# The table of attention biases is made beside the first norm and stored from 128 partitions instead of 8

## The chip, the cores and the metric

The kernel runs on one core of a Trainium2 chip. The metric is the device time of one execution in microseconds (us). Five engines work side by side, each through its own list of instructions in a fixed order: PE multiplies matrices, ACT (ScalarE), DVE (VectorE) and POOL (GpSimd) compute on the on-chip memory, and SP (SyncE) here only issues transfers (DMAs). An instruction starts when those before it on its engine have been issued and the semaphores it waits for have come.

## The reference, cut to what matters

Two transformer-like blocks follow one another on 1024 tokens of width 1024. The first one normalises `x`, projects it by `w_in`, and feeds two branches: attention in a window, and a state-space scan. Here is the part of it that the change touches:

```
h = rms_norm(x, norm_gain);  q, k, v, ... = split(h @ w_in)
rel  = (arange(384) - 128)[None, :] - arange(128)[:, None]        # key minus query
bias = rel_table[t5_bucket(rel)]                                  # (128, 384, 8 heads)
scores = where(|rel| <= 128 and key in range, q @ k.T / 8 + bias, -1e30)
m = max(scores.max(-1), sink);  p = exp(scores - m)
out = (p / (p.sum(-1) + exp(sink - m))) @ v                       # per block of 128 queries
```

The bias depends on key minus query alone. So for each head one row of 512 numbers (relative positions -255 to 256, with -1e30 where the window ends) holds all of it, and query `q` needs 384 of them from `127 - q` on.

The rest of the first block (gates, scan, merge), the modulation vectors of the second block, and the whole second block (a scan, a short convolution and a layer of experts) follow the same reference in both kernels.

## The kernel before

`phase_a` (L340) does the first block's projections, attention and scan. It loads `x` in eight tiles of 128 tokens (L350). `norm_T` (L303) normalises them in two groups of four tiles and writes the transposed result, split into a high and a low part, as `hTh` and `hTl`: ACT squares and sums (`junk`, L309), DVE finds the inverse roots (`rst`, `rsy`) and scales (`xn`, L315), PE transposes (`nps`, L321), ACT evacuates (`nz`, L324), DVE rounds (`hTh`, L268), POOL subtracts (`hTl`, L269).

The projection takes 34 weight pieces of 512 KB. Each is loaded into one of two `raw` buffers (L258) and split by ACT (`whi`, L266) and POOL (`wlo`, L269); 48 matmuls on it fill two halves of 512 tokens (L277 to L279). Pieces 0 to 5 give `kT`, `v` and the four `qT` (matmuls named `pqkv`); the other 28 (`prest`) are used as filler between the steps of attention and of the scan (`k.fill`).

`attention` (L432) first makes the table. `tab` (32 rows, one more for the mask, by 8 heads) times the one-hot matrix `oh` (33 x 512) gives `pb`, 8 heads x 512 positions; DVE copies it to `fb`. One DMA (L447) stores that to memory as `d_f`, 128 copies of each head's row at a pitch of 513 numbers: 1024 rows of 2 KB, read from 8 partitions. A second DMA (L449) reads `d_f` with the pitch 512, so that partition `q` gets its row shifted by `q`: this is `bt`, 128 x 8 x 384. Every score tile adds its part of `bt` on DVE while it takes the maximum (`sc`, L469).

`modulation` (L840) sums 48 pieces of `ada_w` (512 KB each, two buffers, also named `raw`, L861) on DVE into `ac` (L863), two sums per piece for the first 16 pieces and one for the others; column sums of these (`pm`, L868) go through PE.

The order of instructions on each engine isn't written out by hand. A scheduler takes the program, simulates a timeline of it, and puts each engine's instructions into the order in which the simulation would start them; the order is fixed when the kernel is built. All transfers named here are issued by SP, one after the other.

Of the kernel before, what the change touches and what calls it, by code (L numbers as in the profile page):

```python
# [7 lines left out]
F32 = mybir.dt.float32  # L8
# [4 lines left out]
AF = mybir.ActivationFunctionType  # L13
# [146 lines left out]
class K:  # L160
# [25 lines left out]
    def pool(s, name, side="left", tags=""):  # L186
        return Pool(s.tc, name, side, tags)
# [113 lines left out]
def norm_T(k, pool, xs, ntile, scale, bias, hi, lo):  # L301

    nc = k.nc  # L303
    G = min(4, ntile)
    for g in range(ntile // G):
        ms = pool.tile([128, G], F32, tag=f"nms{G}", name="ms", bufs=2)
        junk = pool.tile([128, 1024], F32, tag="njunk", name="junk", bufs=1)
        for t in range(G):
            nc.scalar.activation(junk, xs[g * G + t], AF.Square, accum_out=ms[:, t:t + 1])  # L309
        nc.vector.tensor_scalar(ms, ms, 1.0 / 1024, 1e-6, op0=OP.mult, op1=OP.add)  # L310
        r = k.rsqrt(pool, ms, G)
        xn = []
        for t in range(G):
            z = pool.tile([128, 1024], F32, tag="nxn", name="xn", bufs=5)
            nc.vector.tensor_scalar(z, xs[g * G + t], r[:, t:t + 1], None, op0=OP.mult)  # L315
            xn.append(z)
        W = 128 * G
        for c in range(8):
            ps = k.sm("nps")
            for t in range(G):  # L320
                nc.tensor.transpose(ps[:, 128 * t:128 * t + 128], xn[t][:, 128 * c:128 * c + 128], k.ident)  # L321
            z = pool.tile([128, 512], F32, tag="nz", name="nz", bufs=3)[:, :W]
            if bias is None:
                nc.scalar.activation(z, ps[:, :W], AF.Copy, scale=scale[:, c:c + 1])  # L324
            else:
                nc.scalar.activation(z, ps[:, :W], AF.Identity, scale=scale[:, c:c + 1], bias=bias[:, c:c + 1])
            k.split(hi[:, c, g * W:(g + 1) * W], lo[:, c, g * W:(g + 1) * W], z, he="dve")
# [5 lines left out]
def phase_a(k):  # L333

    nc, tc, A = k.nc, k.tc, k.A
    act, stt = nc.scalar.activation, nc.vector.scalar_tensor_tensor
    d4 = lambda n: k.dp.tile([4, 128, 1024], F32, name=n)
    k.d_za, k.d_zs, k.d_att, k.d_ys, k.d_u = d4("d_za"), d4("d_zs"), d4("d_att"), d4("d_ys"), d4("d_u")
    k.d_g = k.dp.tile([8, 128, 2, 1024], F32, name="d_g")
    with ExitStack() as cx:  # L340
        pool = lambda c, n, **kw: c.enter_context(k.pool(n, **kw))
        k.streams(pool(cx, "ws", side="right", tags="raw whi wlo"), 2, 2, 2)
        hp = pool(cx, "hT", side="right")
        hT = hp.tile([128, 8, 1024], F32R, name="hTh")
        lT = hp.tile([128, 8, 1024], F32R, name="hTl")
        with k.pool("n1") as n1:
            xs = []
            for t in range(8):
                z = n1.tile([128, 1024], F32, tag="x", bufs=8, name="x")
                nc.sync.dma_start(z, A["x"][128 * t:128 * t + 128, :])  # L350
                xs.append(z)
            norm_T(k, n1, xs, 8, k.vs("norm_gain"), None, hT, lT)
        ev = pool(cx, "ev", tags="ev")

        def rest():

            for i in range(28):
                wh, wl = k.piece(A["w_in"][6 + i])
                for sl in H2:
                    ps = k.proj(wh, wl, hT, lT, sl, name="prest")  # L360
                    t = ev.tile([128, 512], F32, tag="ev", bufs=2, name="ev")
                    if i < 4:

                        act(t.rearrange("p (j n) -> p j n", j=8), ps.rearrange("p (n j) -> p j n", j=8), AF.Copy)
                        n0 = sl.start // 8
                        nc.sync.dma_start(k.d_u[i].rearrange("p (j n) -> p j n", j=8)[:, :, n0:n0 + 64],
                                          t.rearrange("p (j n) -> p j n", j=8))
                    elif i < 12:

                        act(t, ps, AF.Tanh, scale=0.5)  # L370
                        stt(t, t, 1.0, ps, op0=OP.add, op1=OP.mult)
                        nc.sync.dma_start((k.d_za, k.d_zs)[(i - 4) // 4][i % 4, :, sl], t)
                    else:

                        m, c = i % 2, (i - 12) // 2
                        act(t, ps, AF.Tanh, scale=0.5, bias=k.h("b_gate", 8 * m + c))  # L376
                        nc.sync.dma_start(k.d_g[c, :, m, sl], t)
                    yield

        todo = rest()  # L380

        def fill(n, after=None):

            with ExitStack() as c:
                if after is not None:
                    c.enter_context(tc.issue_after(after.ins))
                for _ in range(n):
                    next(todo, None)

        k.fill = fill  # L390
        sc = cx.enter_context(tc.tile_pool(name="sc", bufs=1))

        with ExitStack() as ca:
            at = pool(ca, "at")
            qT = at.tile([128, 4, 1024], F32, name="qT")
            kT = at.tile([128, 1024], F32, name="kT")
            vt = at.tile([128, 8, 128], F32, name="vt")
            for j in range(6):
                wh, wl = k.piece(A["w_in"][j])
                for sl in H2:  # L400
                    ps = k.proj(wh, wl, hT, lT, sl, name="pqkv")
                    if j == 0:
                        act(kT[:, sl], ps, AF.Copy)
                    elif j == 1:
                        v = at.tile([128, 512], F32, tag="o", bufs=2, name="v")
                        act(v, ps, AF.Copy)
                        pv = k.sm("pv")
                        for t in range(4):
                            nc.tensor.transpose(pv[:, 128 * t:128 * t + 128], v[:, 128 * t:128 * t + 128], k.ident)
                        act(vt[:, sl.start // 128:sl.stop // 128], pv, AF.Copy)  # L410
                    else:
                        act(qT[:, j - 2, sl], ps, AF.Copy, scale=0.125)
            k.dbg("qT", qT)
            k.dbg("kT", kT)
            k.dbg("vt", vt)
            attention(k, at, qT, kT, vt)
            with k.pool("md") as md:
                modulation(k, md)
            with k.pool("s0") as s0:
                C = ssm_consts(k, sc, s0)  # L420
        k.psum(f=2, acc=1, sm=2, g=2)
        y2 = pool(cx, "y2").tile([128, 4, 1024], F32, name="y2")
        with k.pool("sq") as sq:
            for qt in range(4):
                ssm_quarter(k, sq, C, qt, y2)
        k.psum(f=2, acc=1, sm=4)
        k.dbg("y2", y2)
        glu(k, y2)
        k.fill(99)


def attention(k, at, qT, kT, vt):  # L432
    nc, tc, A = k.nc, k.tc, k.A
    ident = k.ident

    tab = at.tile([33, 8], F32, name="tab")
    nc.gpsimd.memset(tab, -1e30)
    nc.sync.dma_start(tab[0:32, :], A["table"])
    oh = at.tile([33, 512], F32, name="oh")
    nc.sync.dma_start(oh, A["onehot"])  # L440
    ps = k.sm("pb")
    nc.tensor.matmul(ps[0:8, :], tab, oh, start=True, stop=True)
    fb = at.tile([8, 512], F32, name="fb")
    nc.vector.tensor_copy(fb, ps[0:8, :])

    d_f = k.dp.tile([8, 128 * 513], F32, name="d_f")
    nc.sync.dma_start(d_f.rearrange("h (q i) -> h q i", i=513)[:, :, 0:512], fb[:, None, :].to_broadcast([8, 128, 512]))  # L447
    bt = at.tile([128, 8, 384], F32, name="bt")
    nc.sync.dma_start(bt, bass.AP(tensor=d_f.tensor, offset=d_f.offset + 127, ap=[[512, 128], [128 * 513, 8], [1, 384]]))  # L449
    sink = at.tile([128, 8], F32, name="sink")  # L450
# [1 line left out]
    for n in range(8):  # L452
# [8 lines left out]
        for i in range(4):  # L461
            pss = [k.g("psc") for _ in range(2)]
            for g in range(2):
                rows = slice(64 * g, 64 * g + 64)
# [1392 lines left out]
def program(ctx, tc, A, out, dbg=None):  # L1857
    k = K(ctx, tc, A, dbg)
    phase_a(k)
    rec = rwkv(k)  # L1860
    with ExitStack() as rx:
        k.streams(rx.enter_context(k.pool("wsb", "right", "raw whi wlo")), 2, 3, 3)
        with k.pool("hc") as hc:
            k.hc = [hc.tile([128, 8, 256], F32R, name=n) for n in ("hch", "hcl")]
            h, l = merge(k, rx)
            in_proj_2(k, h, l)
        next(rec)
        conv(k, h, l)
    next(rec)
    with ExitStack() as lc:  # L1870
        d_x3 = moe(k, lc)
    last_norm(k, d_x3, out)
# [21 lines left out]
```

## Time and profile before

| | us |
|---|---|
| three timed runs | 2776.07, 2783.78, 2784.15 (median 2783.78) |
| the profiled execution's own time | 2789.1 |
| its span in the profile | 2787.3 |
| PE busy in the span | 2415.8 (87%) |
| DVE busy in the span | 1749.9 (63%) |
| ACT busy in the span | 1169.7 (42%) |

The profile's times are counted from the start of the span. A share of busy time is a mean over stages with different limits; PE's matmuls overlap, so their durations add up to more than their starts are apart. [...]

### The profile page before, as it was taken

Reading aid. Unit: us, or ns where it says so; the run is one execution under the profiler, and the core shown is the slowest. Engines: PE = TensorE matmul, PEld = TensorE weight load, DVE = VectorE, ACT = ScalarE, POOL = GpSimd, SP = SyncE. Lnnn points to the kernel's source line nnn. Section 1 sums busy time; section 2 is a strip of 40 time slices with the busy share of each in tenths; the row PEclk is TensorE's granted clock in tenths of the full one; section 3 lists DMA queues with packets and bytes.
Section 4 is the critical chain, followed back from the end, with each engine's and each line's share of the span. In section 5 each row is a group of like instructions: output and inputs, shape, how many; then the busy total and the mean of one; then the engine's idle time right before and its main releaser. Section 6 shows DMA issues by size and latency. Waiting matters only on the chain.

```text
span 2787.3 us, 40281 instructions
## 1 busy us (share of the span) xinstructions
PE 2415.8 (87%) x15678; PEld 1994.3 (72%) x15678; DVE 1749.9 (63%) x2728; ACT 1169.7 (42%) x1893; POOL 770.4 (28%) x696
## 2 busy tenths in 40 slices
PE   5789998888689995998998698889995999999994
PEld 4566777766577994787787577767874888777873
DVE  7064636766523347222566986784676999888986
ACT  3123332222222133323626546543232776666764
POOL 5111123442335337342423312343320011101110
PEclk8969998788899997998997566568986999999997
DMA  5354322111253423444313122255646999999994
GB/s 182 53 183 157 111 72 69 38 58 45 75 181 129 164 76 124 135 142 153 105 39 91 58 62 61 69 164 176 214 157 243 356 371 375 338 341 340 373 328 170
DMA packets 220283, 458.52 MB, mean 165 GB/s; under 512 B 45632, under 2 KB 139904, under 8 KB 195517
## 3 DMA queue, kind: packets, MB, share of 16 engines
q1 hardware_dynamic: 203868, 406.80, 42.4%
q0 software_dynamic: 6240, 21.10, 2.8%
q10 hardware_dynamic: 9984, 28.05, 2.5%
q8 instruction: 123, 2.02, 0.3%
q14 instruction: 68, 0.55, 0.1%
HBM read 370.03 MB, written 77.22 MB: 160 GB/s over the span
## 4 chain that ended last, share of the span: by engine, by line
PE 54%; DVE 20%; issue 6%; DMA 5%; ACT 5%; POOL 3%; SPq 0%; ACTq 0%; DVEq 0%; POOLq 0%
PE px L277 2%; PE px L278 2%; PE pg L1797 2%; PE px L279 2%; PE pg L1795 2%; PE pg L1796 2%; PE prest L277 2%; PE prest L278 2%; PE prest L279 2%; PE pu L1796 2%; PE pu L1795 2%; PE pu L1797 1%; PE pcv L278 1%; PE pcv L277 1%; PE pcv L279 1%
## 5 line engine op out<-in xcount | busy, mean ns | idle before, releaser
L266 ACT ACTIVATE whi<-raw 128x2048 fp32r<-128x2048 f32 (+1 forms) x279 | 458.6, 1650 | 496.2 <-PE prest L278 94.8
L269 DVE TENSOR_TENSOR wlo<-raw,whi 128x2048 fp32r<-128x2048 f32 x192 | 435.9, 2288 | 57.8 <-ACT whi L266 50.3
L269 POOL TENSOR_TENSOR wlo<-raw,whi 128x1024 fp32r<-128x1024 f32 x87 | 215.6, 2481 | 506.2 <-ACT whi L266 487.3
L277 PE MATMUL prest<-hTh,whi 128*128 128x512 f32 x448 | 183.2, 409 | 5.2 <-ACT ev L376 5.2
L278 PE MATMUL prest<-hTl,whi 128*128 128x512 f32 x448 | 179.8, 401 | 0.0
L279 PE MATMUL prest<-hTh,wlo 128*128 128x512 f32 x448 | 179.5, 401 | 0.0
L1818 POOL DMA_INDIRECT d_x<-o,ids x16 | 52.2, 3261 | 418.2 <-DVE o L1817 418.2
L863 DVE SCALAR_TENSOR_TENSOR ac<-raw,sc,ac 128x1024 f32<-128x1024 f32 x64 | 94.0, 1483 | 30.8 <-DMA raw<-in_ada_w 25.7
L1795 PE MATMUL pg<-whi,xth 128*128 128x512 f32 x256 | 104.7, 409 | 6.4 <-ACT xth L1783 6.4
L277 PEld LDWEIGHTS prest<-hTh,whi 128*128 128x128 f32 x448 | 88.0, 196 | 24.9 <-ACT ev L376 6.0
L1797 PE MATMUL pg<-whi,xtl 128*128 128x512 f32 x256 | 104.6, 409 | 0.0
L1796 PE MATMUL pg<-wlo,xth 128*128 128x512 f32 x256 | 103.7, 405 | 0.0
L1796 PE MATMUL pd<-wlo,hth 128*128 128x512 f32 x256 | 100.8, 394 | 0.3 <-DVE wlo L269 0.3
L279 PEld LDWEIGHTS prest<-hTh,wlo 128*128 128x128 f32 x448 | 87.1, 194 | 18.9
L278 PEld LDWEIGHTS prest<-hTl,whi 128*128 128x128 f32 x448 | 87.5, 195 | 17.7
L1796 PE MATMUL pu<-wlo,xth 128*128 128x512 f32 x256 | 100.1, 391 | 0.0
L1795 PE MATMUL pu<-whi,xth 128*128 128x512 f32 x256 | 100.0, 390 | 0.0
L1797 PE MATMUL pd<-whi,htl 128*128 128x512 f32 x256 | 99.8, 390 | 0.0
L1797 PE MATMUL pu<-whi,xtl 128*128 128x512 f32 x256 | 99.7, 389 | 0.0
L1031 DVE SCALAR_TENSOR_TENSOR mix<-px,omu,mix 128x1024 f32<-128x1024 f32 (+1 forms) x23 | 23.2, 1014 | 114.2 <-ACT mix L1030 110.8
L469 DVE CUSTOM_DVE_ANT_0 sc<-psc,bt 128x384 f32<-128x384 f32 (+1 forms) x64 | 32.7, 520 | 98.1 <-DMA bt<-d_f 52.2
L277 PE MATMUL px<-h2h,whi 128*128 128x512 f32 x224 | 89.9, 402 | 1.2 <-ACT px L1022 1.2
(581 smaller groups left out, 6828.7 us busy)
## 6 DMA issues: line engine op xcount, KB each, us to landing
raw<-in_w_g SPq DMA_DIRECT2D x64, 1024.0 KB, 10.9
raw<-in_w_u SPq DMA_DIRECT2D x64, 1024.0 KB, 7.7
raw<-in_w_d SPq DMA_DIRECT2D x64, 1024.0 KB, 7.3
raw<-in_w_in SPq DMA_DIRECT2D x69, 512.0 KB, 3.7
raw<-in_ada_w SPq DMA_DIRECT2D x48, 512.0 KB, 3.6
x<-in_x SPq DMA_DIRECT2D x16, 512.0 KB, 5.6
d_g<-ev SPq DMA_DIRECT2D x32, 256.0 KB, 3.2
gt<-d_g SPq DMA_DIRECT2D x16, 512.0 KB, 4.8
```

The lines of the kernel that those rows point to most:

```text
L266: nc.scalar.activation(hi, src, AF.Copy)
L269: (nc.gpsimd if le == "pool" else nc.vector).tensor_tensor(lo, src, hi.bitcast(F32), op=OP.subtract)
L277: mm(ps, wh[:, c], xh[:, kt, sl], start=kt == 0, stop=False)
L278: mm(ps, wh[:, c], xl[:, kt, sl], start=False, stop=False)
L279: mm(ps, wl[:, c], xh[:, kt, sl], start=False, stop=kt == kts - 1)
L469: nc.vector.tensor_tensor_reduce(sc[:, :W], pss[g][:, :W], bt[:, 4 * g + i, c0:c1], 1.0, -3e38, op0=OP.add, op1=OP.max, accum_out=MX[g][:, ...
L863: nc.vector.scalar_tensor_tensor(ac, raw, sc[:, 8 * w + p:8 * w + p + 1], ac, op0=OP.mult, op1=OP.add)
L1031: nc.vector.scalar_tensor_tensor(xv, body[:, :, 0:W], k.omu[:, mu:mu + 1], xv, op0=OP.mult, op1=OP.add)
L1795: mm(o, h[:, kt], wh[:, c], start=kt == 0, stop=False)
L1796: mm(o, h[:, kt], wl[:, c], start=False, stop=False)
L1797: mm(o, l[:, kt], wh[:, c], start=False, stop=kt == 7)
L1818: nc.gpsimd.indirect_dma_start(out=d_x3, out_offset=bass.IndirectOffsetOnAxis(ap=ids[:, :1], axis=0), in_=o, in_offset=None, compute_op=OP ...
```

## The change

A new function `bias_table` makes the table, and `phase_a` calls it after the loads of `x` and before `norm_T`. Each column of `tab` is repeated 16 times by a copy on POOL (`trep`, 33 x 128), so the same matmul now gives 128 rows, 16 for each head. ACT evacuates them instead of DVE. The store writes the same 1024 rows of `d_f`, but takes eight of them from each of the 128 partitions. `attention` only reads `bt` and `sink`. The tiles `tab`, `oh`, `trep` and `fb` lie in the pool of the norm instead of that of attention.

```
             for t in range(8):
                 z = n1.tile([128, 1024], F32, tag="x", bufs=8, name="x")
                 nc.sync.dma_start(z, A["x"][128 * t:128 * t + 128, :])
                 xs.append(z)
+            bias_table(k, n1)
             norm_T(k, n1, xs, 8, k.vs("norm_gain"), None, hT, lT)
...
+def bias_table(k, pool):
+    nc, A = k.nc, k.A
+    tab = pool.tile([33, 8], F32, name="tab")
+    nc.gpsimd.memset(tab, -1e30)
+    nc.sync.dma_start(tab[0:32, :], A["table"])
+    oh = pool.tile([33, 512], F32, name="oh")
+    nc.sync.dma_start(oh, A["onehot"])
+    rep = pool.tile([33, 8, 16], F32, name="trep")
+    nc.gpsimd.tensor_copy(rep, tab[:, :, None].to_broadcast([33, 8, 16]))
+    ps = k.sm("pb")
+    nc.tensor.matmul(ps, rep.rearrange("p h r -> p (h r)"), oh, start=True, stop=True)
+    fb = pool.tile([128, 512], F32, name="fb")
+    nc.scalar.activation(fb, ps, AF.Copy)
+
+    d_f = k.d_f = k.dp.tile([8, 128 * 513], F32, name="d_f")
+    rows = d_f.rearrange("h (r s i) -> (h r) s i", s=8, i=513)
+    nc.sync.dma_start(rows[:, :, 0:512], fb[:, None, :].to_broadcast([128, 8, 512]))
...
-    ps = k.sm("pb")
-    nc.tensor.matmul(ps[0:8, :], tab, oh, start=True, stop=True)
-    fb = at.tile([8, 512], F32, name="fb")
-    nc.vector.tensor_copy(fb, ps[0:8, :])
-    d_f = k.dp.tile([8, 128 * 513], F32, name="d_f")
-    nc.sync.dma_start(d_f.rearrange("h (q i) -> h q i", i=513)[:, :, 0:512], fb[:, None, :].to_broadcast([8, 128, 512]))
+    ident, d_f = k.ident, k.d_f
     bt = at.tile([128, 8, 384], F32, name="bt")
     nc.sync.dma_start(bt, bass.AP(tensor=d_f.tensor, offset=d_f.offset + 127, ap=[[512, 128], [128 * 513, 8], [1, 384]]))
```

The scheduler orders the whole program anew. Lines of the changed kernel are 1 higher than before up to the new function and 8 higher from L449 of before on. Three places matter most.

SP's list before, where the table is stored (pieces of `w_in` and `ada_w` are the loads around it):

```order
L440 DMA oh<-in_onehot 33x512
L438 DMA tab<-in_table 32x8
L861 DMA raw<-in_ada_w 128x1024 x2
L258 DMA raw<-in_w_in 128x1024
L857 DMA ac<-in_ada_b 1x1024
L258 DMA raw<-in_w_in 128x1024 x2
L447 DMA d_f<-fb 1024x1x512
L449 DMA bt<-d_f 128x8x384
L258 DMA raw<-in_w_in 128x1024 x3
```

SP's list after the change, from the loads of `x` on:

```order
L350 DMA x<-in_x 128x1024 x8
L438 DMA tab<-in_table 32x8
L440 DMA oh<-in_onehot 33x512
L258 DMA raw<-in_w_in 128x1024 x2
L865 DMA ac<-in_ada_b 1x1024 x2
L869 DMA raw<-in_ada_w 128x1024 x2
L450 DMA d_f<-fb 1024x1x512
L258 DMA raw<-in_w_in 128x1024
L869 DMA raw<-in_ada_w 128x1024
L258 DMA raw<-in_w_in 128x1024
L869 DMA raw<-in_ada_w 128x1024
L569 DMA wz<-in_perm 128x352
```

The store has moved ahead of all but two pieces of each weight, and between it and the read of `bt` (below the rows shown) there are now twelve other loads, where before there was none.

DVE's list before, from the last sums of the norm's stage to the first score tiles:

```order
L869 COPY cm<-pm 128x8
L879 COPY n_2690<-cm 128x8
L863 SCALAR_TENSOR_TENSOR ac<-raw,sc,ac 128x1024 x2
L444 COPY fb<-pb 8x512
L469 ISA sc,mx<-psc,bt 128x256
L469 ISA mx 128x1
L469 ISA sc,mx<-psc,bt 128x256
L469 ISA mx 128x1
```

The same place after the change:

```order
L877 COPY cm<-pm 128x8
L887 COPY n_2699<-cm 128x8
L871 SCALAR_TENSOR_TENSOR ac<-raw,sc,ac 128x1024 x2
L877 COPY cm<-pm 128x8
L887 COPY n_2699<-cm 128x8
L871 SCALAR_TENSOR_TENSOR ac<-raw,sc,ac 128x1024 x8
L477 ISA sc,mx<-psc,bt 128x256
L477 ISA mx 128x1
L871 SCALAR_TENSOR_TENSOR ac<-raw,sc,ac 128x1024 x6
L477 ISA sc,mx<-psc,bt 128x256
```

The copy of `fb` is gone from DVE, and fourteen more sums of the modulation stand ahead of the second score tile: eight ahead of the first and six between the two.

ACT's list after the change, from the squares of the norm on (before, two `nz` stood between the two `whi`, and there was no `fb`):

```order
L309 ACTIVATE junk,ms<-x 128x1024 x8
L266 ACTIVATE whi<-raw 128x1024
L446 ACTIVATE fb<-pb 128x512
L266 ACTIVATE whi<-raw 128x1024
L324 ACTIVATE nz<-nps,vec 128x512 x11
L404 ACTIVATE kT<-pqkv 128x512
```

The evacuation of `fb` and the second `whi` now stand ahead of the first `nz`.

## Rows read from the trace of the kernel before

**Rows 1.** The page's first line: the span of the profiled execution.
```profile
span 2787.3 us, 40281 instructions
```
**Rows 2.** Busy us by engine (instructions) per stretch; PE clock, DMA share, GB/s.
```profile
66.50:122.00 55.50, 55.36 (x247) 43.75 (x245) 5.04 (x6) 11.20 (x16) 14.17 (x7) 1.00 0.34 62
122.00:146.00 24.00, 0.05 (x1) 0.00 (x0) 0.24 (x1) 0.00 (x0) 0.00 (x0) 0.60 0.56 120
146.00:172.00 26.00, 24.90 (x73) 15.92 (x74) 19.90 (x51) 7.43 (x25) 3.31 (x2) 0.51 0.40 141
182.00:190.00 8.00, 7.86 (x29) 6.31 (x28) 5.16 (x12) 4.26 (x17) 0.00 (x0) 0.50 0.39 129
146.00:440.00 294.00, 277.67 (x1328) 207.97 (x1330) 155.86 (x448) 99.61 (x262) 46.80 (x48) 0.89 0.40 127
```
**Rows 3.** Waits from 0 to 440 us: who for whom; total, times, longest.
```profile
DVE sc L469 <- DMA bt<-d_f: 52.2, 1, 52.2
...
PE psc L465 <- DVE mx L469: 32.4, 7, 24.2
...
ACT whi L266 <- DMA raw<-in_w_in: 30.6, 1, 30.6
```
**Rows 4.** Timeline of SP: start, duration, what was issued.
```profile
78.68 11.56 SPq L258 DMA_DIRECT2D raw<-in_w_in  x2
93.63 0.83 SPq L447 DMA_DIRECT2D d_f<-fb  x1
138.14 0.39 SPq L449 DMA_DIRECT2D bt<-d_f  x1
138.63 0.99 SPq L258 DMA_DIRECT2D raw<-in_w_in  x2
```
**Rows 5.** Timeline of PE around the gap: start, duration, instructions, idle before.
```profile
121.66 0.39 PE L279 MATMUL pqkv<-hTh,wlo 128*128 128x512 f32 x1
146.24 1.56 PE L465 MATMUL psc<-kT,qT 64*128 64x256 f32 x4 [24.20 <-DVE mx L469]
```
**Rows 6.** Timeline of DVE at the end of the gap.
```profile
145.75 0.42 DVE L469 CUSTOM_DVE_ANT_0 sc<-psc,bt 128x256 f32<-128x256 f32 x1 [52.15 <-DMA bt<-d_f]
```
**Rows 7.** DMA from 95 to 137 us: packets, then SP's queue with its share.
```profile
DMA packets 1009, 2.08 MB, mean 50 GB/s; under 512 B 0, under 2 KB 0, under 8 KB 1008
...
q1 hardware_dynamic: 1008, 2.06, 45.4%
```
**Rows 8.** DMA issues over the whole span: KB each, median us to landing.
```profile
raw<-in_w_g SPq DMA_DIRECT2D x64, 1024.0 KB, 10.9
...
raw<-in_ada_w SPq DMA_DIRECT2D x48, 512.0 KB, 3.6
...
d_x<-x SPq DMA_DIRECT2D x8, 512.0 KB, 2.7
```
**Rows 9.** Timeline of ACT from the first weight piece on.
```profile
16.21 1.06 ACT L266 ACTIVATE whi<-raw 128x1024 fp32r<-128x1024 f32 x1
17.34 1.27 ACT L324 ACTIVATE nz<-nps,vec 128x512 f32<-128x512 f32 x2
18.50 1.06 ACT L266 ACTIVATE whi<-raw 128x1024 fp32r<-128x1024 f32 x1
```
**Rows 10.** Timeline of DVE: the first sums of the modulation.
```profile
23.68 4.66 DVE L863 SCALAR_TENSOR_TENSOR ac<-raw,sc,ac 128x1024 f32<-128x1024 f32 x2
```
**Rows 11.** Groups on DVE from 20 to 66 us: count, busy us, mean ns, idle.
```profile
L863 DVE SCALAR_TENSOR_TENSOR ac<-raw,sc,ac 128x1024 f32<-128x1024 f32 x16 | 27.3, 1730 | 0.0
L268 DVE CAST hTh<-nz 128x512 fp32r<-128x512 f32 x15 | 10.4, 701 | 0.0
L315 DVE TENSOR_SCALAR xn<-x,rsy 128x1024 f32<-128x1024 f32 x4 | 4.8, 1249 | 0.0
```
**Rows 12.** Timeline of PE: the table's matmul.
```profile
91.87 1.02 PE L442 MATMUL pb<-oh,tab 33*8 33x512 f32 x2
```
**Rows 13.** Groups from 146 to 440 us: the modulation's sums.
```profile
L863 DVE SCALAR_TENSOR_TENSOR ac<-raw,sc,ac 128x1024 f32<-128x1024 f32 x46 | 63.5, 1391 | 29.3 <-DMA raw<-in_ada_w 25.7 <-DMA ac<-in_ada_b 3.4
```

More of the change, by code (lines that the diff above doesn't have):

```diff
@@ L429, in phase_a @@
         k.fill(99)
+def bias_table(k, pool):
[14 more added lines that the diff above has]
+    nc.sync.dma_start(rows[:, :, 0:512], fb[:, None, :].to_broadcast([128, 8, 512]))
 def attention(k, at, qT, kT, vt):
     nc, tc, A = k.nc, k.tc, k.A
[L434 to L440, printed above, removed]
-    ps = k.sm("pb")
-    nc.tensor.matmul(ps[0:8, :], tab, oh, start=True, stop=True)
-    fb = at.tile([8, 512], F32, name="fb")
-    nc.vector.tensor_copy(fb, ps[0:8, :])
-    d_f = k.dp.tile([8, 128 * 513], F32, name="d_f")
-    nc.sync.dma_start(d_f.rearrange("h (q i) -> h q i", i=513)[:, :, 0:512], fb[:, None, :].to_broadcast([8, 128, 512]))
+    ident, d_f = k.ident, k.d_f
     bt = at.tile([128, 8, 384], F32, name="bt")
```

## The prediction

> **What bounds the kernel now.** I read the stretches first. From 66.5 to 122 us PE works without a pause at the full clock, on the matmuls `pqkv`; from 122 to 146 it does nothing; from 146 to 172 it is busy again, but at a clock of 0.51 [rows 2]. So there is one hole of 24 us, early, with work on both sides of it. The timeline of PE dates it: the last matmul of the projection starts at 121.66, and the next instruction, a score matmul, has stood idle for 24.20 us when it starts at 146.24 [rows 5].
>
> Then the waits, for who ends it. PE waits for DVE, whose score tiles hold the accumulators that the next `psc` needs, and DVE waits 52.2 us for `bt` [rows 3], until 145.75 [rows 6]. ACT at the same time waits 30.6 us for a weight piece [rows 3], and the last `qT` stands behind that split. All three come from SP: it issues the store of `d_f` at 93.63 and then nothing until 138.14, when `bt`, which reads `d_f`, can go, and the pieces behind it at 138.63 [rows 4]. The store takes 44.5 us (138.14 - 93.63), the read of `bt` another 7.6 (145.75 - 138.14). While the store runs alone, SP's queue keeps 45.4% of the 16 DMA engines busy, about 7.3 of them, at 50 GB/s [rows 7].
>
> **The change, part by part.** *The gap.* The first attention tile no longer needs a store issued at 93.6. `d_f` is issued in the first 20 us, and `bt` is read as soon as the tiles of the norm are free, near 60 us by the place it has in SP's list. That removes 24.2 us of idle PE [rows 5]. What is late next is PE itself: the last `pqkv` at 122, since it has no idle time from 66.5 on [rows 2]. DVE's 52 us are not the gain; only the 24.2 are.
>
> *The store.* Trace and change differ in the number of source partitions. No row has this store from 128. Above, it can take the 44.5 us that it takes now. Below, the nearest row is a store of 512 KB from 128 partitions, 2.7 us [rows 8]; four of them make 10.8. I take 11, because that row has the same kind of source, and keep both ends. [...]
>
> *What stands behind the store.* SP's loads share its queue; no row has loads behind this store, and I count as if those issued after it land after it. It is issued when `fb` is ready: the first split starts at 16.21, the next ACT instruction at 17.34, and an evacuation of 128 x 512 takes half of 1.27 [rows 9], so at 18.0. Behind it come one piece of `w_in` and the third piece of `ada_w`, each 3.6 us [rows 8]: the latter lands at 18.0 + T + 7.2. DVE needs it after four sums, seven casts and four `xn`, 4 x 1.73 + 7 x 0.70 + 4 x 1.25 = 16.8 us [rows 11] after the first sum, which starts at 23.68 [rows 10]: at 40.5. So DVE stalls for T - 15.3: not at all at 11 (4.3 us to spare), 7 us at 22, 29 us at 44.5. I take 0.
>
> *The start.* `tab` and `oh` are loaded behind `x` and cost the small time of 67 KB. The matmul moves from a stretch where PE is full, where it holds it for 1.02 us less the overlap of its end, 0.8 [rows 12], to the time before the first transposes. POOL's copy comes before its first `wlo`, when it is idle. On ACT, `fb` (0.6) and the second split (1.1) now stand ahead of the first `nz` [rows 9]: the norm starts up to 1.7 us later. The split only changes places with two `nz`, so the lower bound is 0.6; I take 1.7, since PE's first matmuls hang on the first `nz`.
>
> *The clock.* After the gap PE runs 26 us at half speed, 24.9 us of them busy [rows 2]. If all of that ran at full speed, 12.5 us would be saved; if the stage is held by the chain from score to softmax to transpose, nothing. The row for 182 to 190 shows PE at half clock again, long after the gap [rows 2], so the stage brings its own low clock. I take a third, 4.
>
> *The sums.* Fourteen sums of the modulation are pulled ahead of the second score tile. At 1.39 us each [rows 13] they are 19.5 us of DVE, which before had 52 us idle there [rows 6]. In the attention stage they lighten DVE, but it isn't the bound there (155.9 of 294 us busy [rows 2]): 0 for the sum.
>
> *The rest* (2.3 ms) is the same work, in an order that the scheduler has drawn anew in small places. No row prices that; I take 0 and give the own range several us on either side for it.
>
> **Sum.** 24.2 + 0.8 + 4 - 1.7 = 27.3 us less. The profiled execution took 2789.1 us (span 2787.3 [rows 1]), so 2761.8 by its own time; it is 5.3 us above the median of the runs, and from 2783.8 the sum gives 2756.5. I say 2757, own range 2745 to 2769.
>
> **Rivals.** *A larger gain.* Attention starts warm and the sums are ahead, so the 12.5 us of the clock come in full, and half of the 16.3 us of PE's idle time from 146 to 440 (294 - 277.7 [rows 2]) goes with DVE's waits for `ada_w`, 25.7 us [rows 13]. 24.2 + 0.8 - 1.7 + 12.5 + 8 = 44: 2740. For it: PE was cold where it was busiest. Against it: the clock row at 182.
>
> *The store doesn't get faster.* If the width of the source isn't what holds it (the odd pitch of 2052 bytes stays), T is 44.5 and the idle time only moves: DVE stands 29 us in the norm, 2757 + 29 = 2786, no change that a measurement of this kernel tells (0.3%, 8.4 us). For it: every packet waits in the same place in memory as before. Against it: eight of sixteen engines were idle. [...]
>
> *Slower: the sums become the wait.* The second score tile now stands behind fourteen sums on DVE, two per piece, and their seven loads stand in SP's list behind weight pieces that go out from 78.7 to 90 us [rows 4]. If they start at 79 and a piece takes 3.6 + 2 x 1.39 = 6.4 us one after the other, the sums end at 124, 2 us behind PE; overlapped, 16 us ahead of it. At 10.9 us a piece, as the loads of `w_g` take in a crowded queue [rows 8], they end at 155: 33 us late, 24.2 given back, 2784 + 33 - 24.2 + 0.9 = 2794. It turns slower from 9.6 us a piece on ((146 - 79)/7). For it: two buffers only, and SP's list is in order. Against it: `ada_w` lands in 3.6 us, and the DMA engines are 34% busy there, mostly with the store that leaves [rows 2].
>
> **How the numbers follow.** Forecast 0.66; larger gain 0.12; unchanged store 0.10; late sums 0.12, from 2769 up to 2796, of which 0.08 beyond 2792, 0.02 within 0.3% and 0.02 faster. Faster by over 0.3%: 0.66 + 0.12 + 0.02 = 0.80. Within: 0.10 + 0.02 = 0.12. Slower: 0.08. The range 2740 to 2778 leaves out the unchanged store and nearly all of the late sums, about 0.2.
>
> **What would show it.** Right: no wait for `bt` on DVE; the store under 15 us; no hole in PE's timeline near 120 us; the last `pqkv` near 123 and the first softmax right behind it. Wrong: DVE idle between 30 and 60 us, before an `ac` (the store is slow); PE idle near 120 with DVE in sums (the sums are late); PE's last `pqkv` well after 125 (the norm was disturbed); or the gap gone and the later stages longer by as much.

## The result, and the profile after

The changed kernel takes 2741.86 us (median of 4 runs, 2739.39 to 2745.42), the kernel before 2783.97 on the same chip (2776.07 to 2790.56). The ratio is 0.9851, with a 95% interval of 0.9834 to 0.9868: 42 us faster, where 27 were forecast. The time lies inside the range of 2740 to 2778, but under the forecast's own range of 2745 to 2769, and next to the rival called "a larger gain" (2740).

Busy time by stretch, cut at events that both kernels have: the start of the last `pqkv`, of the first and of the last `oT` (the end of the first block of attention and of the last one), of the last `V` on DVE, and of the first store of `d_ys`. Columns as in [rows 2], PE's granted clock as a share of full speed. Before:

```profile
0.00:121.70 121.70, 93.20 (x384) 70.48 (x384) 60.30 (x83) 35.78 (x54) 49.43 (x31) 0.92 0.43 128
121.70:201.60 79.90, 54.08 (x209) 38.83 (x207) 40.03 (x88) 16.04 (x50) 7.59 (x4) 0.66 0.49 145
201.60:434.20 232.60, 222.71 (x1117) 168.21 (x1115) 110.28 (x356) 82.88 (x211) 36.00 (x43) 0.95 0.38 120
434.20:603.00 168.80, 139.82 (x922) 116.75 (x923) 122.81 (x187) 39.22 (x65) 72.41 (x92) 0.80 0.14 46
603.00:763.80 160.80, 123.37 (x732) 102.01 (x731) 98.89 (x153) 39.55 (x59) 55.10 (x58) 0.85 0.17 58
```

After:

```profile
0.00:126.10 126.10, 96.18 (x399) 72.35 (x400) 81.57 (x104) 36.38 (x55) 51.70 (x33) 0.93 0.59 184
126.10:173.70 47.60, 44.05 (x191) 30.95 (x189) 20.38 (x60) 17.36 (x53) 6.53 (x4) 0.78 0.39 120
173.70:397.90 224.20, 216.48 (x1119) 165.13 (x1117) 108.06 (x360) 82.58 (x210) 34.00 (x42) 0.96 0.38 116
397.90:568.50 170.60, 144.69 (x922) 120.64 (x923) 119.61 (x186) 39.33 (x65) 72.91 (x92) 0.78 0.14 45
568.50:719.90 151.40, 121.86 (x732) 100.60 (x731) 100.64 (x155) 39.64 (x59) 54.55 (x58) 0.87 0.19 61
```

The second column of each row is the length of the stretch. Their differences are +4.4, -32.3, -8.4, +1.8 and -9.4: together -43.9, and from there to the last store the two kernels run level (the last `out` is issued at 2782.4 and at 2738.6). Only the -32.3 holds the hole of 24.20 [rows 5]; 8.1 us of it are more than the hole. So the gain is four pieces: the hole without the later start (-24.2 + 4.4), the first block (-8.1), the rest of attention (-8.4), the scan (-7.6).

The same stretch up to the last `pqkv` for DVE's sums alone (the lines with `ac`; DVE busy with its count, then PE's clock, DMA share, GB/s), before and after:

```profile
0.00:121.70 121.70, 30.53 (x18) 0.92 0.43 128
```

```profile
0.00:126.10 126.10, 52.44 (x32) 0.93 0.59 184
```

Fourteen more of the 64 sums are done before attention starts, as the prediction read from the order.

The wait for `bt` [rows 3, 6] is gone from the list of waits of after, where the longest wait of a score tile is now for its own matmul (8.4 us). SP's timeline (the counterpart of [rows 4]) and PE's at the old hole ([rows 5]):

```profile
20.29 0.64 SPq L450 DMA_DIRECT2D d_f<-fb  x1
...
64.39 0.39 SPq L457 DMA_DIRECT2D bt<-d_f  x1
```

```profile
126.10 0.39 PE L279 MATMUL pqkv<-hTh,wlo 128*128 128x512 f32 x1
126.42 0.70 PE L473 MATMUL psc<-kT,qT 64*128 64x256 f32 x4
```

The next score matmul follows the projection in 0.32 us; no idle time stands in its row. DMA from 20.5 to 33 us (as [rows 7]):

```profile
DMA packets 1043, 2.16 MB, mean 173 GB/s; under 512 B 14, under 2 KB 14, under 8 KB 1043
...
q1 hardware_dynamic: 1043, 2.16, 97.8%
```

The 2.1 MB of the store need about these 12.5 us, with the 16 engines 97.8% busy, where 44.5 us at 45.4% stood before. What the early place costs is in the waits of the first 30 us:

```profile
PE pb L444 <- POOL trep L442: 17.6, 1, 17.6
...
POOL trep L442 <- DMA tab<-in_table: 14.1, 1, 14.1
```

`pb` is PE's first matmul in the new order, and the transposes of the norm stand behind it in PE's list: the first `nps` starts at 19.6 instead of 14.8.

### The profile page after: what moved, and what is told of

It is laid out like the page before. It is cut to its first block, busy times and chain, and to the rows that moved or that the text cites. A ratio compares the mean times of both kernels' runs of the same rounds, so it can differ in the third digit from the quotient of the medians.

```text
span 2743.6 us, 40289 instructions
## 1 busy us (share of the span) xinstructions
PE 2397.9 (87%) x15678; PEld 1980.9 (72%) x15678; DVE 1754.1 (64%) x2727; ACT 1173.5 (43%) x1894; POOL 771.7 (28%) x697
## 4 chain that ended last, share of the span: by engine, by line
PE 51%; DVE 22%; issue 6%; ACT 6%; DMA 5%; POOL 3%; SPq 0%; ACTq 0%; DVEq 0%; POOLq 0%
PE px L277 2%; PE px L278 2%; PE px L279 2%; PE pg L1805 2%; PE pg L1803 2%; PE pg L1804 2%; PE pu L1804 2%; PE pu L1803 2%; PE pu L1805 2%; DVE wlo L269 1%; PE prest L277 1%; PE prest L278 1%; PE prest L279 1%; DMA raw<-in_w_d 1%; PE po L495 1%
## 5 line engine op out<-in xcount | busy, mean ns | idle before, releaser
L1803 PE MATMUL pd<-whi,hth 128*128 128x512 f32 x256 | 89.9, 390 | 0.3 <-DVE o L1825 0.3
```

Of the source, the lines that this page charges most:

```text
L1803: mm(o, h[:, kt], wh[:, c], start=kt == 0, stop=False)
```

## The experiments

All times are medians in us, ratios are against runs of the kernel before on the same chip. The stretches are those of the two tables above, read from each kernel's trace by the same events. What follows the first store of `d_ys` is the same work in all of them and takes 2006.5 to 2026.7 us in the single traces, so the stretches of one trace and the median of its kernel needn't agree to better than that spread.

| kernel | median | ratio, 95% interval | last pqkv | to first oT | to last oT | to last V | to d_ys |
|---|---|---|---|---|---|---|---|
| before | 2783.97 | | 121.7 | 79.9 | 232.6 | 168.8 | 160.8 |
| changed | 2741.86 | 0.9851, 0.9834 to 0.9868 | 126.1 | 47.6 | 224.2 | 170.6 | 151.4 |
| width alone | 2764.78 | 0.9928, 0.9905 to 0.9952 | 123.7 | 53.9 | 235.3 | 169.2 | 161.0 |
| place alone | 2767.53 | 0.9943, 0.9926 to 0.9959 | 147.3 | 47.5 | 225.4 | 168.0 | 161.4 |
| even pitch | 2740.59 | 0.9849, 0.9833 to 0.9866 | 125.0 | 47.0 | 224.1 | 170.6 | 151.5 |
| 16 partitions | 2745.53 | 0.9856, 0.9839 to 0.9872 | 129.6 | 46.3 | 226.8 | 169.1 | 161.5 |
| sums held | 2759.26 | 0.9915, 0.9885 to 0.9945 | 126.0 | 58.1 | 230.7 | 172.3 | 153.3 |
| scan order | 2789.54 | 1.0009, 0.9989 to 1.0029 | 123.9 | 81.6 | 233.4 | 171.4 | 156.6 |
| stride | 2744.45 | 0.9856, 0.9829 to 0.9882 | 123.9 | 43.2 | 224.4 | 173.9 | 158.9 |
| after the norm | 2755.48 | 0.9890, 0.9850 to 0.9930 | 123.6 | 42.9 | 232.8 | 167.9 | 161.1 |
| more sums | 2753.85 | 0.9874, 0.9840 to 0.9908 | 140.4 | 42.7 | 222.7 | 169.8 | 156.5 |
| scan put back | 2740.32 | 0.9872, 0.9834 to 0.9910 | 126.5 | 47.5 | 224.0 | 168.0 | 151.5 |

My theory at the start was the prediction's: the hole goes because the store is short and early, and the rest is the clock. The rivals: one half of the change would do alone; or the gains behind the hole have nothing to do with it.

**Width alone.** The store keeps its old place.

```
+    rep = at.tile([33, 8, 16], F32, name="trep")
+    nc.gpsimd.tensor_copy(rep, tab[:, :, None].to_broadcast([33, 8, 16]))
-    nc.tensor.matmul(ps[0:8, :], tab, oh, start=True, stop=True)
+    nc.tensor.matmul(ps, rep.rearrange("p h r -> p (h r)"), oh, start=True, stop=True)
...
+    rows = d_f.rearrange("h (r s i) -> (h r) s i", s=8, i=513)
+    nc.sync.dma_start(rows[:, :, 0:512], fb[:, None, :].to_broadcast([128, 8, 512]))
```

> Width alone: the table stays in its old place in attention, but is multiplied out to 128 rows and stored from 128 partitions. Theory (the width shortens the store, and the short store alone removes the hole): issued near 93.6 us as before, the store takes about 13.5 us as in the changed kernel, bt lands near 115 us, ahead of the last pqkv at 121.7, so the hole of 24.2 us is gone though nothing was moved; the gain is 24 us plus what the attention stage gives back, 2745 to 2756. If all 42 us come with the hole, 2743; if those beyond the hole belong to the sums that moved ahead, 2756 (24.2 + some 4 off 2783.8). Rival (the width does nothing, the changed kernel's store is short because the DMA engines are free at 20 us): the store takes 44 us, the hole stays, 2784.

Its time is 2764.78, past the upper end of 2756. SP's and DVE's timeline:

```profile
95.67 0.64 SPq L451 DMA_DIRECT2D d_f<-fb  x1
110.58 0.38 SPq L453 DMA_DIRECT2D bt<-d_f  x1
```

```profile
117.68 0.42 DVE L473 CUSTOM_DVE_ANT_0 sc<-psc,bt 128x256 f32<-128x256 f32 x1 [22.04 <-DMA bt<-d_f]
```

The store takes 14.9 us at the latest (110.58 - 95.67), `bt` is there at 117.68, 6 us ahead of the last `pqkv`, and the hole is closed: 79.9 - 53.9 = 26.0 us in that stretch. Nothing else is gained: the start is 2.0 us later, the rest of attention 2.7 us longer, and the scan as long as before, which leaves 20.7 us up to `d_ys`. So the width alone closes the hole, and 17 of the 42 us (by the medians) are there by it; the others came with the early place.

**Place alone.** The changed kernel, but `fb` has 8 rows and the store reads 8 partitions.

```
-    fb = pool.tile([128, 512], F32, name="fb")
+    fb = pool.tile([8, 512], F32, name="fb")
...
+    nc.sync.dma_start(d_f.rearrange("h (q i) -> h q i", i=513)[:, :, 0:512], fb[:, None, :].to_broadcast([8, 128, 512]))
```

> Place alone: the table is made beside the first norm, but stored from 8 partitions as before. Theory (loads issued behind the store on SP's queue land behind it, and 8 source partitions hold it at 44 us): issued near 19 us it ends near 63, the third piece of ada_w lands near 70 us, DVE stands some 29 us in the norm, and the last pqkv comes some 25 to 29 us later than in the changed kernel: 2765 to 2775, so of the 42 us a part of 10 to 20 is left. Rival 1 (the loads are not held back): the store is hidden, 2742 as with both. Rival 2 (in the early place 8 partitions are no slower, since nothing else loads): the store takes about 14 us, 2742.

2767.53. The stall is where the prediction's "unchanged store" put it, on DVE in the norm, behind the third piece of `ada_w`:

```profile
67.64 2.48 DVE L868 SCALAR_TENSOR_TENSOR ac<-raw,sc,ac 128x1024 f32<-128x1024 f32 x2 [25.83 <-DMA raw<-in_ada_w]
```

T - 15.3 gives 29.2 us for T = 44.5; 25.8 were measured, and the last `pqkv` is 25.6 us later than before. Still the kernel is faster than before by 0.6%: first block and rest of attention are as short as in the changed kernel (47.5 and 225.4). SP shows what the loads behind the store do:

```profile
19.67 0.82 SPq L447 DMA_DIRECT2D d_f<-fb  x1
21.64 13.72 SPq L258 DMA_DIRECT2D raw<-in_w_in  x1
35.45 4.59 SPq L866 DMA_DIRECT2D raw<-in_ada_w  x1
```

The issue of the next load holds SP itself for 13.7 us, and those after it for 4.6 each, against 0.42 in the changed kernel.

**Even pitch, and 16 partitions.** Both are the changed kernel with one number changed: rows 528 numbers apart (2112 bytes) instead of 513, or 16 rows of `fb` with 64 stores from each. Of each the fence shows the lines that set it.

```
-    d_f = k.d_f = k.dp.tile([8, 128 * 513], F32, name="d_f")
+    d_f = k.d_f = k.dp.tile([8, 128 * 528], F32, name="d_f")
```

```
-    rows = d_f.rearrange("h (r s i) -> (h r) s i", s=8, i=513)
-    nc.sync.dma_start(rows[:, :, 0:512], fb[:, None, :].to_broadcast([128, 8, 512]))
+    rows = d_f.rearrange("h (r s i) -> (h r) s i", s=64, i=513)
+    nc.sync.dma_start(rows[:, :, 0:512], fb[:, None, :].to_broadcast([16, 64, 512]))
```

> The changed kernel with rows of d_f 2112 bytes apart instead of 2052, so that each packet of 2 KB begins on a multiple of 64 bytes. Theory (the DMA engines move the packets of an even write at the price of the 512 KB store of the trace before, 2.7 us): the store falls from 13 to 14 us to 11 or less. Rival (the place in memory does not matter, the sixteen engines' own rate holds it): 13 to 14 us as before. Either way the store is hidden by 15.3 us of cover, and the time is 2742 within 4 us.

> The changed kernel with the store from 16 partitions, 64 rows of 2 KB from each, instead of 128 partitions with 8 rows each. Theory (what counts is how many DMA engines the outer dimension feeds, 16 at most): 13 to 14 us as with 128, and 2742. Rival (it counts how many partitions of the tile are read at once): twice the 8 partitions give half of 44.5 us, 22 us, DVE then waits 7 us or less in the norm, 2742 to 2749.

DMA of the even pitch from 20.5 to 26 us (the first row in 40 slices), then of 16 partitions from 21 to 41:

```profile
GB/s 0 0 104 387 372 402 402 343 417 357 387 432 343 417 357 372 417 313 432 343 387 432 357 402 417 357 402 372 372 417 343 417 387 372 387 283 313 268 194 223
DMA packets 920, 1.88 MB, mean 343 GB/s; under 512 B 0, under 2 KB 0, under 8 KB 920
```

```profile
DMA packets 957, 1.97 MB, mean 98 GB/s; under 512 B 0, under 2 KB 0, under 8 KB 956
## 3 DMA queue, kind: packets, MB, share of 16 engines
q1 hardware_dynamic: 956, 1.96, 92.7%
```

At the even pitch the slices stand near 385 GB/s up to the last five, where they fall to some 200; 1.88 of the 2.1 MB are through at 26, and at 200 GB/s the rest takes one more us. So the store takes some 6 us from its first packet at 20.8, and the theory was right. At 16 partitions it takes 21 us (2.1 MB / 98 GB/s) with the 16 engines 92.7% busy, where the changed kernel has 12.5 us at 97.8%: the rival was right, the number of busy engines is not what set the time. The wait is there too: DVE stands 5.06 us for the third piece of `ada_w`, where T - 15.3 gives 6. The times agree with the changed kernel's: a store of 6 to 13 us is hidden, and one of 21 nearly.

**Stride.** Eight partitions again, but 4 apart (`fb` has 32 rows, and every fourth is stored), and the even pitch; and, as a second kernel, the one before with the even pitch alone, whose code isn't shown.

```
+    rows = d_f.rearrange("h (q i) -> h q i", i=528)
+    nc.sync.dma_start(rows[:, :, 0:512], fb[0:32:4, None, :].to_broadcast([8, 128, 512]))
```

> The changed kernel with 2112 byte rows, stored from 8 partitions that lie 4 apart (0, 4, ... 28), 128 rows from each. Theory A (a partition is read by one transfer at a fixed rate, so the number of partitions sets the time): 44 us as from 8 neighbours, and DVE waits some 26 us in the norm. [...]

> The kernel before with rows of d_f 2112 bytes apart instead of 2052: 8 neighbouring partitions, old place, even rows. Theory (with 8 partitions the reading side holds the store, and the odd rows only matter once that is lifted): 44.5 us from the issue of d_f to that of bt, the hole stays, 2783 within 4 us. Rival (the odd rows cost the same 8 us, 13.5 less 5.5, whoever reads): 36 us, a hole of 16, 2775.

DMA of the first from 20.5 to 24.3 us, and of the second from 97 to 139:

```profile
DMA packets 375, 0.77 MB, mean 202 GB/s; under 512 B 0, under 2 KB 0, under 8 KB 375
...
q1 hardware_dynamic: 375, 0.77, 52.6%
```

```profile
DMA packets 1002, 2.06 MB, mean 49 GB/s; under 512 B 2, under 2 KB 2, under 8 KB 1001
```

Eight partitions give 49 GB/s as neighbours and 202 with a stride of 4: which partitions, not how many. The 202 come with the engines 52.6% busy, where 16 neighbouring partitions had 98 at 92.7%. Theory A fell: at 202 GB/s the 2.1 MB are 10.4 us, where it had 44, and DVE's longest wait for a piece of `ada_w` is 2.4 us, where it had some 26. The first kernel was run once here, with 2731.32. The second, also run once, has 2781.88: its store takes 45.3 us from issue to issue, and the hole stays, as its theory said.

**The sums held back.** The changed kernel, with the fourteen sums that had moved ahead of the score tiles kept behind the fourth, and the scan's order pinned by its fillers.

```
+                if n == 0 and i == 1 and g == 1:
+                    k.held = r
...
+                if j == 1 and p >= 1:
+                    c.enter_context(tc.issue_after(k.held.ins))
```

> The changed kernel, but the fourteen sums of the modulation that had moved ahead of the second score tile are held until the fourth score tile has been read, as they stood in the kernel before; the order of the last quarter of the scan (WI ahead of the prest pieces) is pinned to that of the changed kernel, so that only the sums differ. Theory (of the 42 us, some 15 in attention came from the sums leaving it): the last pqkv at 124 to 126, the first block, from there to the first oT, 54 us instead of 47.6, the rest of attention 232 to 235 instead of 224, the scan end 151.5 as it was; 2742 + 6 + 8 to 11 = 2756 to 2760. Rival (the attention stage is shorter because it starts warm and without a hole; the sums are free, DVE not being the bound there): 2742 within 3 us.

2759.26: 17 us of the 42 are lost. In attention the trace has 10.5 more in the first block (the theory had 6) and 6.5 more in the rest (8 to 11); the scan is 3.6 us longer as well, so its order wasn't pinned in full. From the last `pqkv` to the last `oT` it takes 288.8 us; the kernel before without its hole takes 79.9 + 232.6 - 24.2 = 288.3, the changed kernel 271.8. DVE's timeline of the first block, then that of the changed kernel:

```profile
127.37 4.60 DVE L878 SCALAR_TENSOR_TENSOR ac<-raw,sc,ac 128x1024 f32<-128x1024 f32 x2
131.90 0.41 DVE L477 CUSTOM_DVE_ANT_0 sc<-psc,bt 128x256 f32<-128x256 f32 x1
...
132.58 2.47 DVE L878 SCALAR_TENSOR_TENSOR ac<-raw,sc,ac 128x1024 f32<-128x1024 f32 x2
134.97 0.41 DVE L477 CUSTOM_DVE_ANT_0 sc<-psc,bt 128x256 f32<-128x256 f32 x1
...
135.66 0.27 DVE L485 TENSOR_TENSOR nm<-mx,sink 128x4 f32<-128x4 f32 x2
```

```profile
127.50 0.42 DVE L477 CUSTOM_DVE_ANT_0 sc<-psc,bt 128x256 f32<-128x256 f32 x1
...
130.58 0.16 DVE L483 TENSOR_TENSOR nm<-mx,sink 128x4 f32<-128x4 f32 x1
```

With the sums between the score tiles the first row maximum `nm`, for which ACT's exponentials wait (8.5 us in the changed kernel, in three waits), comes 9.7 us after the last `pqkv`, without them 4.5.

This isn't the order of the kernel before, though, as the expectation had it. There, and with width alone, the eight score tiles of the first block stand ahead of any further sum; here the sums stand behind the fourth. DVE with width alone:

```profile
129.11 0.16 DVE L479 TENSOR_TENSOR nm<-mx,sink 128x4 f32<-128x4 f32 x1
...
131.08 1.28 DVE L867 SCALAR_TENSOR_TENSOR ac<-raw,sc,ac 128x1024 f32<-128x1024 f32 x1 [1.07 <-DMA ac<-in_ada_b]
```

`nm` comes 5.4 us after the last `pqkv` there, and still the two stretches take 289.2 us. So the run shows that these fourteen sums, left in attention, can cost 17 us. It doesn't show that the kernel before paid them through a late first `nm`.

**The table after the norm.** The changed kernel with the call moved one line down; the scheduler then leaves the fourteen sums where they were, inside attention.

```
-            bias_table(k, n1)
             norm_T(k, n1, xs, 8, k.vs("norm_gain"), None, hT, lT)
+            bias_table(k, n1)
```

> The changed kernel with the table made behind the first norm instead of beside it, in the text; the scheduler then leaves the fourteen sums where they stood before (18 ahead of the first score tile, 19 ahead of the twelfth). Theory (the place has three separate effects: it delays the norm by 4 us, it lets the fourteen sums go ahead, which is worth 16.5 us in attention, and it draws a new order in the scan): without any of them the time is that of width alone, 2764, with the last pqkv at 122 to 124, 55 to 58 us from there to the first oT, 231 to 235 for the rest of attention. Rival (the early, warm start of attention itself is worth the 16.5 us): 2745 to 2750.

2755.48, with a wide spread (2739.63 to 2773.46), and neither of the two. The start is regained as expected (last `pqkv` at 123.6, first `nps` at 16.3). But the first block takes 42.9 us where the theory had 55 to 58, though 18 sums stand ahead of attention as in the kernel before:

```profile
124.66 0.42 DVE L477 CUSTOM_DVE_ANT_0 sc<-psc,bt 128x256 f32<-128x256 f32 x1 [5.87 <-PE psc L473]
...
128.34 0.16 DVE L483 TENSOR_TENSOR nm<-mx,sink 128x4 f32<-128x4 f32 x1
```

`nm` comes 4.7 us after the last `pqkv`. Both stretches together take 275.7 us, 12.6 less than the kernel before without its hole, and 3.9 more than the changed kernel. So my theory that a sum costs 1.2 us wherever it stands in attention fell. What goes with the length of the first block is how many sums run inside it. For width alone, the changed kernel and the table after the norm (length, DVE busy on sums with their count, PE's clock, DMA share, GB/s):

```profile
123.70:177.60 53.90, 28.05 (x21) 0.75 0.45 144
```

```profile
126.10:173.70 47.60, 10.28 (x8) 0.78 0.39 120
```

```profile
123.60:166.50 42.90, 17.35 (x14) 0.80 0.41 131
```

In all traces without a hole, 8 to 14 sums go with 42.7 to 47.6 us, and 21 with 53.9 and 58.1 (the kernel before: 22, and 55.7 without its hole). Below 14 the count doesn't order the lengths. The clock moves along in the main, from 0.68 with the sums held to 0.88 with more sums ahead, so how much of the price is waiting and how much is the clock isn't told apart.

**More sums ahead, and the stride kernel timed.** In the stride kernel, the first 24 loads of `ada_w` and their 40 sums are put ahead of the projection in the text.

```
+            with k.pool("md", side="right") as md:
+                mod = modulation(k, md)
+                next(mod)
+                for j in range(6):
+                    wh, wl = k.piece(A["w_in"][j])
...
+        if j == 3:
+            yield
```

> The kernel of the stride experiment with the first 24 loads of the modulation, and their 40 sums, ahead of the projection in the text; 40 instead of 32 sums then stand ahead of the third score tile, and some small work of the scan's constants moves into the norm too. Theory (a sum that leaves the attention stage gives back 16.5 / 14 = 1.2 us): 8 more give 9 us in attention, first oT to last oT 215 to 220, if the projection keeps its end at 125; 2726 to 2733. Rival (DVE is full ahead of attention, the sums are done at 112 in the changed kernel and 8 more at 1.4 us reach 123, and the small work holds up the norm): the last pqkv moves to 130 or later, and nothing is gained, 2735 to 2750.

> The kernel of the stride experiment again, timed: 8 partitions that lie 4 apart, 2112 byte rows, the early place. One look had 2731.3. Theory (its stages up to attention are those of the changed kernel, and what else it showed is the scheduler's order and the spread of the last 2 ms): 2735 to 2742, no slower than the changed kernel. Rival (it has lost something that the single look hid): 2745 or more.

Both together: the stride kernel has 2744.45 (2739.11 to 2752.05), as fast as the changed one and no faster, so the 2731 was one good execution. With more sums ahead the time is 2753.85: the rival, 4 us past its upper end. DVE is busy for 116 us ahead of the last `pqkv`, which comes at 140.4, and attention gives back 2 us (42.7 + 222.7 = 265.4, against 43.2 + 224.4 = 267.6).

**The order of the scan.** In the kernel before, the fillers of the scan's last quarter, and one from the end of the third, are issued behind `WI`; then, as the opposite, `WI` of the changed kernel is put behind them.

```
+    if qt < 3:
+        k.fill(2, last)
...
+    k.fill(2 if qt < 3 else 5, last)
...
+    if qt != 2:
+        k.fill(1, last)
```

```
+        if qt == 3:
+            c.enter_context(k.tc.issue_after(k.rest.ins))
```

> The kernel before, with one thing changed far from the table: in the last quarter of the scan the prest pieces, which stood between X and WI, are issued behind WI, as the scheduler had drawn them in the changed kernel. Theory (9.4 of the 42 us are this order and have nothing to do with table or store): the stretch from the last V to the first store of d_ys falls from 160.8 to 151.5 us, and 2783 to 2774, while all before it, the hole included, stays. Rival (the stretch is shorter because the core reaches it in another state, or by spread between executions): no change, 2783.

> The changed kernel with WI of the scan's last quarter put behind four prest pieces, as the scheduler had it in the kernel before (there behind three); nothing up to the scan is touched. The counterpart of the scan order experiment. Theory (the 7.5 us that the scan lost, 322.9 from the first to the last V and on to d_ys against 330.4, are this order): 329 to 332 there, 2749. Rival (that experiment gave back only 1.6 us, so the order of WI is a small part, and the rest is the drawn order elsewhere): 323 to 326, 2742 to 2745.

No gain in total for the first (2789.54, interval 0.9989 to 1.0029), though its last stretch is 4.2 us shorter (the one ahead of it is 2.6 longer); and no loss for the second (2740.32), whose scan is as short as the changed kernel's. `WI` is not it. ACT's timeline shows the last `X` of the last quarter, `WI`, and the next thing that waits for PE's result (before, changed, scan put back):

```profile
686.25 0.59 ACT L700 ACTIVATE X<-pv 128x512 f32<-128x512 f32 x1
698.38 1.02 ACT L726 ACTIVATE WI<-pwi 128x1024 f32<-128x1024 f32 x1
736.27 1.15 ACT L266 ACTIVATE yh<-y 128x512 fp32r<-128x512 f32 x2 [25.73 <-PE pyo L788]
```

```profile
638.99 0.60 ACT L708 ACTIVATE X<-pv 128x512 f32<-128x512 f32 x1
643.79 1.03 ACT L734 ACTIVATE WI<-pwi 128x1024 f32<-128x1024 f32 x1 [3.23 <-PE pwi L732]
```

```profile
636.52 0.60 ACT L708 ACTIVATE X<-pv 128x512 f32<-128x512 f32 x1
664.20 1.02 ACT L737 ACTIVATE WI<-pwi 128x1024 f32<-128x1024 f32 x1
```

Counted from the last `V`, this `X` comes at 83.2 to 83.9 us in five orders (before, width alone, place alone, 16 partitions, after the norm), and the stretch is 160.8 to 161.5. At 81 it is 158.3 and 158.9 (the stride kernel, twice), at 77 it is 156.5 and 156.6 (more sums, scan order), at 74.9 it is 153.3 (sums held), at 70.5 it is 151.4 and 151.5 (changed, scan put back, the latter with `WI` 23 us later). In the orders with the late `X` (81 to 84), some 168 `prest` matmuls run between the last `V` and it; where it is early (70 to 77), some 144, half a weight piece fewer. That fits the last `X`, and rules out `WI`; no run moved `X` and nothing else, so the cause of the 9.4 us is likely, and not shown.

## Why the prediction was right, and what it left out

- *The hole.* -24.2 forecast, gone; the width alone closes it, and the place alone only moves it into the norm.
- *The store.* 11 us taken from the row of 512 KB [rows 8], 12.5 measured; with width alone, 14.9 at the latest (from its issue to that of `bt`). That the row came out so close is luck, since it was no measure of the store's parts: from the same 128 partitions the store takes some 6 us at the even pitch, and the odd pitch adds as much.
- *Loads behind the store.* The cover of 15.3 us was right. The stall T - 15.3 was 0 at 12.5 us, 5.06 at 21 (6 worked out), 25.8 at 44.5 (29.2 worked out). No row or run shows the 22 us for which the prediction gives a stall of 7; the nearest is the store from 16 partitions, the one of 21. The rival's price for a store that stays slow, 2786, was too high all the same: place alone takes 2767.53, because its attention is as short as the changed kernel's, a gain that the sum had left at nothing.
- *The start.* +1.7 less 0.8 forecast, +4.4 in the profile. The error is in "tab and oh cost the small time of 67 KB": not their bytes but their place counts. `tab` lands behind `x`, POOL's copy waits for it, PE's first matmul `pb` waits for that until 17.6, and all transposes stand behind `pb`. The four traces with the 128-row table beside the norm have the last `pqkv` at 125.0 to 126.5; five with the old start or the table after the norm have it at 121.7 to 123.9 (the kernel before at even pitch: 123.0). The mean difference is 125.9 - 123.2 = 2.7. How much of a late first transpose is left by then is open: the stride kernel has it at 18.3 and 19.4 too, and its last `pqkv` at 124.4 and 123.9.
- *The clock.* -4 forecast with an upper bound of 12.5. PE's granted clock is 0.78 in the first block, after 0.66 over hole and block. In the kernel with width alone the hole is gone too, the clock there is 0.75 and the block takes 53.9 us, only 1.8 less than the 55.7 (79.9 - 24.2) of before. So the block gains 2 us where the hole alone is gone, less than was put down. What the clock inside the block adds to the effect of the sums is open.
- *The sums.* 0 forecast, because DVE "isn't the bound there". This step failed. Holding them back costs 17 us in all, and 288.8 - 271.8 = 17.0 in attention. DVE's mean share of the stage hid that: the first block is 6 to 15 us longer in the kernels that have 21 sums in it than in those with 8 to 14. By which path is only in part shown: behind the fourth score tile the sums delay `nm`, then ACT, then PE, but in the kernel before they stood behind the eighth. How the 17 us split between the first block and what follows is not sure either: with the table after the norm all of the 12.6 came in the first block, in the changed kernel half of 16.5.
- *Late sums.* The rival on the slower side did not come: in the changed kernel all 32 sums are done at 112.0, 14 us ahead of PE. Where 40 are put ahead, the projection is late.
- *The rest.* 0 forecast; the scan gave 7.6, in an order that the scheduler drew anew far from the edit. It shows in the same size where the last `X` stands as early (even pitch, and with `WI` put back) and is missing or smaller in the others that have the early table.

So the sum of 27.3 held the hole and little else. That the time lies in the range of 2740 to 2778 is owed to the hole and to a range drawn wide enough for the rival, and it holds by 2 us; most of what came beyond the hole belongs to two terms that stood at 0, the sums and the order of the scan. The rival of 0.12, "a larger gain", had the size: it put 20.5 us on the stage of attention, which gave 16.5. Its reason (clock and waits of DVE for `ada_w`) was not the one that the experiments showed.

## What to carry to other kernels

A wait that goes is worth the time until the next thing that is late, and the work that had stood behind it on the waiting engine's list is worth a second look: here holding back fourteen sums that had left attention cost 17 us, where the hole was 24. An instruction put first on an engine's list makes those behind it wait for its own inputs, however small these are: here PE stood for 17.6 us before `pb`, on the way of a table of 1 KB, and the first `nps` came at 19.6 instead of 14.8. Where a scheduler draws the order from a simulation, one edit redraws stages far away; read each stage by events that both kernels have, before a total is put down to the edit.

## What the runs showed of the hardware

- The rate of the store followed the partitions that it reads: 49 GB/s from partitions 0 to 7, 98 from 0 to 15 (at the odd pitch), 202 from 0, 4, ... 28, about 385 from all 128 (most of the store at the even pitch). Why eight partitions that lie 4 apart gave four times the rate of eight neighbours, no run shows.
- At 16 partitions SP's queue kept the 16 engines 92.7% busy at 98 GB/s; from eight partitions 4 apart, 52.6% busy gave 202 GB/s. So in these stores the busy share of the DMA engines was no measure of their rate.
- The pitch of 2052 bytes cost nothing at 49 GB/s (44.5 us from issue to issue, 45.3 at 2112), and about doubled the store from 128 partitions (some 6 us at 2112, 12.5 at 2052).
- Behind the store from 8 partitions the issue of a load held SP: 13.7 us for the first load in the early place, then 4.6 each for the next five, against 0.42 for the first one in the changed kernel.
